# Splitting the weights of the w_a and w_b projections two output tiles at a time

## The chip, the cores and the metric

The kernel runs on one core of one Trainium2 chip. Its time is the device time of the whole program in microseconds (us), the median of several runs. A profile is one execution of the program, recorded instruction by instruction. TensorE is PE there (PEld is its weight load, which overlaps), VectorE is DVE, ScalarE is ACT, SyncE is SP; SP issues nearly all loads.

## The reference, cut to what matters

A two-layer encoder over 512 tokens of width 1024, in float32. In each layer a normed input is projected, four attention heads and four recurrent heads run on it, and their outputs, 512 wide each, are projected back to 1024, gated, added and projected once more:

```python
for layer in range(DEPTH):                       # 2
    h = rmsnorm(x, attn_norm[layer])
    proj = h @ w_in[layer]
    (a_q, a_k, a_v, b_q, b_ff, b_fb, b_i, b_g, gate_a, gate_b) = split_columns(proj)
    y_a = diff_attention(a_q, a_k, a_v, ...) @ w_a[layer]              # w_a: 512 x 1024
    y_b = hgrn2_bidirectional(b_q, b_ff, b_fb, b_i, b_g, ...) @ w_b[layer]   # w_b: 512 x 1024
    merged = jax.nn.sigmoid(gate_a) * y_a + jax.nn.sigmoid(gate_b) * y_b
    x = x + merged @ w_o[layer]                                        # w_o: 1024 x 1024
    h = rmsnorm(x, ffn_norm[layer])
    x = x + (jax.nn.silu(h @ w_gate[layer]) * (h @ w_up[layer])) @ w_down[layer]
return rmsnorm(x, final_norm)
```

## The kernel before, in words

Every large product is made of three matmuls. A float32 operand is split into hi, rounded to the type in which TensorE takes it at full rate, and lo, the rest; `mm3` (lines 207 to 210) adds hi x hi, hi x lo and lo x hi into one PSUM bank. So weights come in three steps. `wload` issues the DMA of up to 2048 columns per partition into a buffer `raw` (two of them). `wsplit` rounds a part of it with ScalarE into `hi` (line 92) and subtracts with VectorE into `lo` (line 81). Then TensorE reads both. The pool of `hi` and `lo` has three buffers each of 128 x 1024, whatever part of them a split fills; a split that needs a fourth waits until TensorE has read the oldest for the last time.

`project_fm` computes output tiles of 128 features x 512 tokens, each in one of four banks (`mbank`, in the trace `m`). With eight blocks of rows (k=8: w_in, w_o) a tile's weights are 8 x 128 = 1024 columns, one full split buffer. With four blocks of rows (k=4: w_a and w_b, whose inputs are 512 wide) they are 512 columns, half a buffer. There are eight such tiles in w_a and eight in w_b, in each of the two layers.

The order of the work is set by the framework's scheduler. It lays the program's instructions out on the engines by their data, their buffers and a priority; what stands under `urgent()` (loads, splits, evictions) goes ahead of the rest. Each engine then runs its list strictly in that order. Within a layer, while the attention runs head by head, TensorE fills in with the second half of gate_b, with w_b (input `obh`, `obl`), with gate_a (input `hh`, `hl`), and at the end with w_a.

The steps at the end of the attention, for the last head: the values' product `ao` (12 matmuls), its square `hsq` and that square's split `sqh`, `sql`, two matmuls with ones into `hss` (lines 398 and 401) that sum it, two activations on `hsq`, the scaling by VectorE (line 84), and the split of the head into `oah` and `oal`. `w_a` sums over the four heads, so each of its tiles has nine matmuls on heads 0 to 2 and three on head 3.

`merge` evicts a tile of w_a: VectorE multiplies it into `ga`, adds that to `gb`, and splits the sum into `mh` (ScalarE) and `ml` (VectorE). These are the eight blocks of rows of w_o, which starts next; its first tiles need `mh` and `ml` of tile 0, and each one all eight in the end.

Of the kernel before, what the change touches and what calls it, by code (L numbers as in the profile page):

```python
# [18 lines left out]
P = 128  # L19
# [28 lines left out]
def kernel(  # L48
# [19 lines left out]
    urgent = tc.high_priority  # L68
# [22 lines left out]
    def split_act(src, hi, lo):  # L91
        return ACT.copy(hi, src), tt(lo, src, hi.bitcast(F32), ALU.subtract)  # L92
# [14 lines left out]
    def bank(name="s"):  # L107
        return pside.tile([P, T], F32, tag="s", name=name)

    def mbank(name="m"):  # L110
        return pm.tile([P, T], F32, tag="m", name=name)
# [76 lines left out]
    def wload(src):  # L188

        _, k, c = src.shape  # L190
        raw = wp.tile([P, 2048], F32, tag="raw", name="raw")
        v = raw[:, :k * c].rearrange("p (k c) -> p k c", c=c)
        load(v, src)
        return v

    def wsplit(v):

        _, k, c = v.shape
        hi = hp.tile([P, 1024], F32R, tag="hi", name="hi")[:, :k * c].rearrange("p (k c) -> p k c", c=c)
        lo = hp.tile([P, 1024], F32R, tag="lo", name="lo")[:, :k * c].rearrange("p (k c) -> p k c", c=c)  # L200
        split_act(v, hi, lo)
        return hi, lo

    def rows(w, k0, nk, c0, n):
        return w[k0 * P:(k0 + nk) * P, c0:c0 + n].rearrange("(k p) c -> p k c", p=P)

    def mm3(ps, lh, ll, rh, rl, start, stop):
        PE.matmul(ps, lh, rh, start=start, stop=False)  # L208
        PE.matmul(ps, lh, rl, start=False, stop=False)  # L209
        PE.matmul(ps, ll, rh, start=False, stop=stop)  # L210

    def project_fm(w, cols, evac, k=DC, ah=None, al=None):

        ah = hh if ah is None else ah
        al = hl if al is None else al
        width = 2048 // k
        i = 0
        while i < len(cols):
            n = 1
            while n * P < width and i + n < len(cols) and cols[i + n] == cols[i] + n * P:  # L220
                n += 1
            with urgent():
                raw = wload(rows(w, 0, k, cols[i], n * P))
            for j in range(n):
                with urgent():
                    wh, wl = wsplit(raw[:, :, j * P:(j + 1) * P])
                ps = mbank()
                for c in range(k):
                    mm3(ps, wh[:, c, :], wl[:, c, :], ah[:, c, :], al[:, c, :], c == 0, c == k - 1)
                with urgent():  # L230
                    evac(i + j, ps)
            i += n
# [30 lines left out]
    with tc.tile_pool(name="init", bufs=1, reuse_waits="tile") as ip:  # L263
# [4 lines left out]
        with urgent():  # L268
            ACT.dma_start(vecs, small)
            for c in range(DC):  # L270
                if c % 4 == 0:
                    raw = wp.tile([P, 2048], F32, tag="raw", name="raw").rearrange("p (k d c) -> p k d c", k=4, d=2)
# [9 lines left out]
        for c in range(DC):  # L282
            with urgent():
# [3 lines left out]
                wh, wl = hi[:, c % 2], lo[:, c % 2]  # L287
# [8 lines left out]
            for i in range(4):  # L296
                cs = slice(i % 2 * P, (i % 2 + 1) * P)
# [6 lines left out]
        with tc.issue_after(norms[-1][1].ins):  # L304
# [53 lines left out]
            for dst, quarter in ((sin, 0.0), (cos, 0.25)):  # L358
                n = ip.tile([P, 32], F32, tag="n", name="n")
# [355 lines left out]
    for l in range(LAYERS):  # L715
        win = w_in[l]
        an = [vecs[:, V_FFN + 8 * l + c:V_FFN + 8 * l + c + 1] for c in range(DC)]
        with ExitStack() as mix:
# [14 lines left out]
            def gate_b(i0):  # L733
                project_fm(win, [G_B + (i0 + i) * P for i in range(4)], scaled(lambda i: gb[:, i0 + i, :]))
                for i in range(i0, i0 + 4):
                    sigmoid(gb[:, i, :])

            with tc.tile_pool(name=f"hgrn{l}", bufs=2, reuse_waits="tile") as hgp:
# [3 lines left out]
                def gates_in(h0):  # L742
                    for h in (h0, h0 + 1):
                        heads[h] = (hgp.tile([P, T], F32, tag="q", name="q"),
                                    hgp.tile([P, 2, T], F32, tag="z", name="z"),
                                    hgp.tile([P, T], F32, tag="sg", name="sg"))
                    if first:
                        with urgent():
                            for i, ps in enumerate(first):
                                scaled(lambda _: heads[i % 2][1][:, i // 2, :])(0, ps)  # L750
                        first.clear()
                    else:
                        for d, c0 in ((0, B_FF), (1, B_FB)):
                            project_fm(win, [c0 + h0 * P, c0 + (h0 + 1) * P],
                                       scaled(lambda i: heads[h0 + i][1][:, d, :]))
                    project_fm(win, [B_Q + h0 * P, B_Q + (h0 + 1) * P], scaled(lambda i: heads[h0 + i][0]))
# [21 lines left out]
            with tc.tile_pool(name=f"merge{l}", bufs=1, reuse_waits="tile") as gm, ExitStack() as late:  # L778
# [11 lines left out]
                with tc.tile_pool(name=f"attn{l}", bufs=1, reuse_waits="tile") as ap:  # L790
# [6 lines left out]
                               k=4, ah=obh, al=obl)  # L797
# [24 lines left out]
        with tc.tile_pool(name=f"ffn{l}", bufs=2, reuse_waits="tile") as fp:  # L822
            gh = fp.tile([P, FC, T], F32R, name="gh", bufs=1)
            gl = fp.tile([P, FC, T], F32R, name="gl", bufs=1)
            for f0 in range(0, FC, 2):
# [3 lines left out]
                for f in (f0, f0 + 1):  # L829
                    c0 = slice((f - f0) * P, (f - f0 + 1) * P)  # L830
                    tmp = []
                    for raw in (rg, ru):
                        with urgent():
                            wh, wl = wsplit(raw[:, :, c0])
                        ps = mbank()
# [14 lines left out]
            if l < LAYERS - 1:  # L850
                nn = [vecs[:, V_ATT + 8 * (l + 1) + c:V_ATT + 8 * (l + 1) + c + 1] for c in range(DC)]
                for c0 in range(0, DC, 2):
                    ps = [mbank(), mbank()]
                    for k0, nk in groups:
                        with urgent():
                            raw = wload(rows(w_down[l], k0, nk, c0 * P, 256))
                        for j in range(2):
                            with urgent():
                                wh, wl = wsplit(raw[:, :, j * P:(j + 1) * P])
# [10 lines left out]
            else:  # L870
# [10 lines left out]
                ps = [[mbank(), mbank()] if t < 2 else [bank(), bank()] for t in range(TC)]  # L881
# [3 lines left out]
                for k, t, half in order:  # L885
                    if k not in sp:
                        with urgent():
                            if k % 2 == 0:
                                raw = wload(rows(w_down[l], k, 2, 0, D))
                            sp[k] = wsplit(raw[:, k % 2:k % 2 + 1, :])  # L890
                    wh, wl = sp[k]
                    tok, cs = slice(t * P, (t + 1) * P), slice(half * 512, (half + 1) * 512)
# [55 lines left out]
```

## Time and profile before

| | us |
|---|---|
| median of 3 runs | 1623.28 |
| lowest and highest run | 1622.96, 1624.02 |
| the profiled execution: its time | 1623.66 |
| the profiled execution: its span, first to last instruction | 1621.9 |
| TensorE busy | 1602.1 |
| VectorE busy | 1013.1 |
| ScalarE busy | 771.6 |

The mean granted TensorE clock of the profiled execution is 0.999. A row of the timeline gives the start of an instruction from the span's start, its duration, engine, line, operation, output <- inputs by the program's names, and in brackets how long the engine had stood idle and what ended that. Matmuls overlap: one lasts 0.39 us, and the next starts before it ends. A row of the waits gives who waited for whom, the total, how many times, and the longest. A row of a window gives busy time and count of each engine in a stretch.

### The profile page before, as it was taken

Reading aid. Unit: us, or ns where it says so; the run is one execution under the profiler, and the core shown is the slowest. Engines: PE = TensorE matmul, PEld = TensorE weight load, DVE = VectorE, ACT = ScalarE, POOL = GpSimd, SP = SyncE. Lnnn points to the kernel's source line nnn. Section 1 sums busy time; section 2 is a strip of 40 time slices with the busy share of each in tenths; the row PEclk is TensorE's granted clock in tenths of the full one; section 3 lists DMA queues with packets and bytes.
Section 4 is the critical chain, followed back from the end, with each engine's and each line's share of the span. In section 5 each row is a group of like instructions: output and inputs, shape, how many; then the busy total and the mean of one; then the engine's idle time right before and its main releaser. Section 6 shows DMA issues by size and latency. Waiting matters only on the chain.

```text
span 1621.9 us, 18719 instructions
## 1 busy us (share of the span) xinstructions
PE 1602.1 (99%) x7456; PEld 1323.5 (82%) x7456; DVE 1013.1 (62%) x1636; ACT 771.6 (48%) x1186; POOL 8.1 (1%) x21
## 2 busy tenths in 40 slices
PE   8999999999999999999999999999999999999998
PEld 6888888887888888888888888888878888888886
DVE  8878977877654444433368789788875444444224
ACT  4666666676432323322355667676754323233213
POOL 2000000000000000000000000000000000000000
PEclk9999999999999999999999999999999999999999
DMA  5312212221333223323322222122123233332221
GB/s 189 105 52 79 79 61 70 78 79 52 104 104 92 90 83 99 111 89 100 103 92 83 73 78 79 54 77 79 52 79 97 84 104 104 104 103 92 104 85 72
DMA packets 117927, 142.53 MB, mean 88 GB/s; under 512 B 3152, under 2 KB 100432, under 8 KB 117840
## 3 DMA queue, kind: packets, MB, share of 16 engines
q1 hardware_dynamic: 117152, 140.78, 26.8%
q8 instruction: 58, 0.95, 0.2%
q10 hardware_dynamic: 688, 0.56, 0.1%
q14 instruction: 29, 0.24, 0.0%
HBM read 139.23 MB, written 2.10 MB: 87 GB/s over the span
## 4 chain that ended last, share of the span: by engine, by line
PE 83%; DVE 11%; ACT 4%; issue 1%; DMA 0%; ACTq 0%; DVEq 0%
PE m L210 24%; PE m L208 24%; PE m L209 24%; DVE lo L81 2%; DVE fl L81 2%; PE sc L542 2%; PE s L208 1%; PE s L209 1%; PE s L210 1%; DVE z L81 1%; PE qk L659 1%; PE wt L706 1%; PE po L593 1%; PE qk L656 1%; DVE cum L447 1%
## 5 line engine op out<-in xcount | busy, mean ns | idle before, releaser
L92 ACT CAST hi<-raw 128x1024 fp32r<-128x1024 f32 (+2 forms) x274 | 272.2, 995 | 616.4 <-PE m L209 477.2
L208 PE MATMUL m<-hh,hi 128*128 128x512 f32 x1216 | 476.5, 392 | 5.7 <-DVE hi L289 5.7
L210 PE MATMUL m<-hh,lo 128*128 128x512 f32 x1216 | 476.2, 392 | 0.0
L209 PE MATMUL m<-hl,hi 128*128 128x512 f32 x1216 | 476.1, 392 | 0.0
L81 DVE TENSOR_TENSOR lo<-raw,hi 128x1024 fp32r<-128x1024 f32 (+2 forms) x282 | 320.9, 1139 | 177.5 <-ACT hi L92 176.1
L208 PEld LDWEIGHTS m<-hh,hi 128*128 128x128 f32 x1216 | 228.9, 188 | 52.2 <-ACT sacc L78 5.7
L209 PEld LDWEIGHTS m<-hl,hi 128*128 128x128 f32 x1216 | 228.9, 188 | 47.3 <-DVE hl L84 0.4
L210 PEld LDWEIGHTS m<-hh,lo 128*128 128x128 f32 x1216 | 228.9, 188 | 47.1 <-DVE lo L81 0.3
L81 DVE TENSOR_TENSOR gu<-m,rbc 128x512 f32<-128x512 f32 x88 | 60.9, 692 | 241.2 <-PE m L210 237.2
L208 PE MATMUL m<-hi,hh 128*128 128x512 f32 x256 | 101.4, 396 | 0.0
L209 PE MATMUL m<-lo,hh 128*128 128x512 f32 x256 | 100.9, 394 | 0.0
L210 PE MATMUL m<-hi,hl 128*128 128x512 f32 x256 | 100.9, 394 | 0.0
L78 ACT ACTIVATE fl<-fl 128x1024 f32<-128x1024 f32 (+1 forms) x56 | 48.5, 872 | 43.8 <-DVE fl L81 43.8
L210 PE MATMUL m<-gh,lo 128*128 128x512 f32 x176 | 68.5, 389 | 0.0
L209 PE MATMUL m<-gl,hi 128*128 128x512 f32 x176 | 68.5, 389 | 0.0
L208 PE MATMUL m<-gh,hi 128*128 128x512 f32 x176 | 68.5, 389 | 0.0
L210 PEld LDWEIGHTS m<-hi,hl 128*128 128x128 f32 x256 | 48.2, 188 | 9.6
L542 PEld LDWEIGHTS sc<-fl 128*128 128x128 f32 x384 | 49.0, 191 | 8.5 <-DVE fl L81 4.3
L209 PEld LDWEIGHTS m<-lo,hh 128*128 128x128 f32 x256 | 48.2, 188 | 9.3
L208 PEld LDWEIGHTS m<-hi,hh 128*128 128x128 f32 x256 | 48.2, 188 | 9.3
L542 PE MATMUL sc<-fl 128*128 128x128 f32 x384 | 51.5, 277 | 2.8 <-DVE fl L81 2.6
L209 PE MATMUL m<-ml,hi 128*128 128x512 f32 x128 | 49.8, 392 | 0.0
(255 smaller groups left out, 2340.4 us busy)
## 6 DMA issues: line engine op xcount, KB each, us to landing
raw<-in_w_in_dram SPq DMA_DIRECT2D x46, 1024.0 KB, 5.0
raw<-in_w_gate_dram SPq DMA_DIRECT2D x22, 1024.0 KB, 5.1
raw<-in_w_up_dram SPq DMA_DIRECT2D x22, 1024.0 KB, 5.1
raw<-in_w_down_dram SPq DMA_DIRECT2D x19, 1024.0 KB, 4.9
raw<-in_w_o_dram SPq DMA_DIRECT2D x8, 1024.0 KB, 4.9
raw<-in_w_b_dram SPq DMA_DIRECT2D x4, 1024.0 KB, 5.0
raw<-in_w_a_dram SPq DMA_DIRECT2D x4, 1024.0 KB, 5.0
raw<-in_w_down_dram SPq DMA_DIRECT2D x4, 768.0 KB, 4.2
```

The lines of the kernel that those rows point to most:

```text
L78: return ACT.activation(o, i, func, **kw)
L81: return DVE.tensor_tensor(o, a, b, op)
L92: return ACT.copy(hi, src), tt(lo, src, hi.bitcast(F32), ALU.subtract)
L208: PE.matmul(ps, lh, rh, start=start, stop=False)
L209: PE.matmul(ps, lh, rl, start=False, stop=False)
L210: PE.matmul(ps, ll, rh, start=False, stop=stop)
L447: DVE.tensor_tensor_scan(row, seg, row, 0.0, ALU.mult, ALU.add)
L542: mm = PE.matmul(ps[:, c], K[:, c], Q[:, c], start=True, stop=True)
L593: mm = PE.matmul(po[:, tok], a, b, start=i == 0, stop=i == len(terms) - 1)
L656: mm = PE.matmul(ps[c], q2[:, c, tok], ka[:, c, :], start=True, stop=False)
L659: PE.matmul(ps[c], q2[:, c, tok], kb[:, c, :], start=False, stop=True)
L706: tr = PE.transpose(pt[:, s * P:(s + 1) * P], w[:, 0, s * P:(s + 1) * P], ident)
```

## The change

For a projection with k blocks of rows, `pair` is the number of output tiles whose weights fill a split buffer: 1 for k=8, 2 for k=4. The split is made once for `pair` tiles, and each tile's matmuls read their half of it. For k=8 nothing changes. For w_a and w_b four splits of 128 x 1024 stand in place of eight of 128 x 512.

```diff
         width = 2048 // k
+        pair = 1024 // (k * P)
         i = 0
@@
             for j in range(n):
-                with urgent():
-                    wh, wl = wsplit(raw[:, :, j * P:(j + 1) * P])
+                if j % pair == 0:
+                    with urgent():
+                        whs, wls = wsplit(raw[:, :, j * P:min(j + pair, n) * P])
+                cs = slice(j % pair * P, (j % pair + 1) * P)
                 ps = mbank()
                 for c in range(k):
-                    mm3(ps, wh[:, c, :], wl[:, c, :], ah[:, c, :], al[:, c, :], c == 0, c == k - 1)
+                    mm3(ps, whs[:, c, cs], wls[:, c, cs], ah[:, c, :], al[:, c, :], c == 0, c == k - 1)
```

The number of matmuls and loads is the same. The scheduler, however, lays out the stretch from the second attention step to the start of w_o anew, in both layers alike; the rest of the program keeps its order. Lines behind the changed ones stand three lower (398 becomes 401, 401 becomes 404). Two places follow, both of layer 0.

The first is TensorE at the end of the attention, between the last `ao` and the first matmul on head 3. Before, from the second sum (L401) on:

```order
L401 MATMUL hss<-sql,ones_r 128x512
L210 MATMUL m<-oah,lo 128x512
L208 MATMUL m<-oah,hi 128x512
L209 MATMUL m<-oal,hi 128x512
L210 MATMUL m<-oah,lo 128x512
L208 MATMUL m<-oah,hi 128x512
L209 MATMUL m<-oal,hi 128x512
L210 MATMUL m<-oah,lo 128x512
L208 MATMUL m<-oah,hi 128x512
L209 MATMUL m<-oal,hi 128x512
L210 MATMUL m<-oah,lo 128x512
L208 MATMUL m<-oah,hi 128x512 x3
```

The ten rows after L401 are w_a on heads 0 to 2; the three in the last row are the first on head 3, one for each of three tiles. Ahead of L401 stand two more of w_a, the first sum, and six of w_a behind the last `ao`. Now the whole stretch, from the last `ao` on:

```order
L210 MATMUL ao<-wh,avl 128x512
L208 MATMUL m<-oah,hi 128x512
L209 MATMUL m<-oal,hi 128x512
L210 MATMUL m<-oah,lo 128x512
L401 MATMUL hss<-sqh,ones_r 128x512
L404 MATMUL hss<-sql,ones_r 128x512
L208 MATMUL m<-oah,hi 128x512 x4
```

Three matmuls of w_a are left between the last `ao` and the first sum, none behind it, and four tiles instead of three wait for head 3. The other matmuls on heads 0 to 2 stand ahead of the last `ao` now.

The second place is the start of w_o. On VectorE, before, with `lo` of w_o's first three blocks (3567, 3600, 3637):

```order
L81 TENSOR_TENSOR lo_3567<-raw_3564,hi_3566 128x1024
L81 TENSOR_TENSOR gb_410<-gb_410,ga_3113 128x512
L81 TENSOR_TENSOR ml_3391<-gb_410,mh_3390 128x512
L81 TENSOR_TENSOR ga_3113<-ga_3113,m_3526 128x512
L81 TENSOR_TENSOR lo_3600<-raw_3564,hi_3599 128x1024
L81 TENSOR_TENSOR gb_410<-gb_410,ga_3113 128x512
L81 TENSOR_TENSOR ga_3113<-ga_3113,m_3547 128x512
L81 TENSOR_TENSOR lo_3637<-raw_3634,hi_3636 128x1024
L81 TENSOR_TENSOR gb_410<-gb_410,ga_3113 128x512
L81 TENSOR_TENSOR ml_3391<-gb_410,mh_3390 128x512 x5
```

Now, from the block before the third one (its numbers are 3568 and 3605):

```order
L81 TENSOR_TENSOR lo_3568<-raw_3532,hi_3567 128x1024
L81 TENSOR_TENSOR gb_410<-gb_410,ga_3097 128x512
L81 TENSOR_TENSOR ml_3375<-gb_410,mh_3374 128x512
L81 TENSOR_TENSOR ga_3097<-ga_3097,m_3515 128x512
L81 TENSOR_TENSOR lo_3605<-raw_3602,hi_3604 128x1024
L81 TENSOR_TENSOR gb_410<-gb_410,ga_3097 128x512
L81 TENSOR_TENSOR ml_3375<-gb_410,mh_3374 128x512 x7
```

One part of `ml` instead of three stands ahead of the third block's `lo`, and seven instead of five behind it. TensorE there, from w_a's last tile (m_3515) on; m_3538, m_3571 and m_3608 are the first three tiles of w_o:

```order
L209 MATMUL m_3515<-oal_2080,hi_3494 128x512
L210 MATMUL m_3515<-oah_2079,lo_3495 128x512
L208 MATMUL m_3538<-mh_3374,hi_3534 128x512
L208 MATMUL m_3571<-mh_3374,hi_3567 128x512
L208 MATMUL m_3608<-mh_3374,hi_3604 128x512
L209 MATMUL m_3538<-ml_3375,hi_3534 128x512
L210 MATMUL m_3538<-mh_3374,lo_3535 128x512
L208 MATMUL m_3538<-mh_3374,hi_3534 128x512
L209 MATMUL m_3571<-ml_3375,hi_3567 128x512
L210 MATMUL m_3571<-mh_3374,lo_3568 128x512
L209 MATMUL m_3538<-ml_3375,hi_3534 128x512
```

hi_3604 takes over the buffer of hi_3494, which w_a's last tile reads until the first of these rows; the last row is the first that needs the second part of `ml`. Before, TensorE took the first three blocks of rows of w_o's first tile, nine matmuls in order, ahead of any other tile, and the third tile only after the first two were done.

## The prediction

> **What bounds the kernel now.** I read the page first, then the waits of TensorE, then the windows around the places that the change touches, and last their timeline.
>
> ```profile
> PE 1602.1 (99%) x7456; PEld 1323.5 (82%) x7456; DVE 1013.1 (62%) x1636; ACT 771.6 (48%) x1186; POOL 8.1 (1%) x21
> PE 83%; DVE 11%; ACT 4%; issue 1%; DMA 0%; ACTq 0%; DVEq 0%
> ```
>
> TensorE is busy 99% of the span, and the chain that ended last runs mostly through it. A change that adds no matmul can therefore change the time only by opening or closing gaps between matmuls. What one matmul costs in a full stream I take from two rows nine matmuls into the same stretch, and the gaps that exist from TensorE's waits:
>
> ```profile
> 386.39 0.39 PE L208 MATMUL m<-oah,hi 128*128 128x512 f32 x1
> 388.20 0.39 PE L210 MATMUL m<-oah,lo 128*128 128x512 f32 x1
> PE m L208 <- DVE hi L289: 5.7, 1, 5.7
> PE sc L542 <- DVE fl L81: 2.6, 3, 1.3
> PE m L210 <- DVE lo L81: 1.8, 2, 0.9
> PE m L208 <- ACT oah L92: 1.2, 2, 0.6
> PE qk L659 <- DVE kb L81: 0.3, 2, 0.2
> ```
>
> From 386.39 to 388.20 there are eight steps: one matmul of 512 columns costs TensorE 0.227 us. Of the waits, the first two lie at the start and in the recurrence, which the change leaves alone. The third and fourth, once in each layer, lie at the w_a projection. So the most that can be won is small, and what can be lost is any stretch where TensorE has nothing independent to do. The windows show where that is already near:
>
> ```profile
> core 0: us, PE busy (x) PEld busy (x) DVE busy (x) ACT busy (x) POOL busy (x), PEclk, DMA share, GB/s
> 272.00:371.60 99.60, 99.48 (x473) 81.40 (x472) 82.67 (x147) 71.84 (x139) 0.00 (x0) 1.00 0.19 64
> 383.40:389.20 5.80, 5.19 (x22) 3.57 (x20) 1.46 (x3) 3.16 (x5) 0.00 (x0) 1.00 0.01 3
> 389.20:394.00 4.80, 3.92 (x16) 2.79 (x17) 3.97 (x7) 2.28 (x4) 0.00 (x0) 1.00 0.00 0
> 394.00:406.20 12.20, 12.20 (x54) 10.10 (x55) 11.99 (x19) 6.14 (x9) 0.00 (x0) 1.00 0.53 173
> 406.20:412.00 5.80, 5.80 (x26) 4.52 (x25) 5.72 (x9) 2.20 (x3) 0.00 (x0) 1.00 0.54 181
> ```
>
> In layer 0 the attention (272 to 371.6) is full. The gaps are in the two windows from 383.4 to 394, where the last attention head is normalised and w_a waits for it. That the waits for lo and oah count 2 each says that layer 1 repeats it.
>
> **The splits themselves.** Sixteen weight blocks are now rounded and subtracted at 1024 columns in place of 32 at 512.
>
> ```profile
> L81 DVE TENSOR_TENSOR lo<-raw,hi 128x1024 fp32r<-128x1024 f32 x234 | 286.0, 1222 | 143.8 <-ACT hi L92 142.3
> L92 ACT CAST hi<-raw 128x1024 fp32r<-128x1024 f32 x234 | 246.0, 1051 | 558.5 <-PE m L209 419.4 <-PE s L210 83.0 <-issue 31.0
> L81 DVE TENSOR_TENSOR lo<-raw,hi 128x512 fp32r<-128x512 f32 x40 | 27.3, 686 | 0.0
> L92 ACT CAST hi<-raw 128x512 fp32r<-128x512 f32 x32 | 19.5, 620 | 22.1 <-PE m L209 22.0
> ```
>
> ScalarE saves 16 x (2 x 0.620 - 1.051) = 3.0 us, VectorE 16 x (2 x 0.686 - 1.222) = 2.4 us. I cost this at nothing: the work is hidden under TensorE, which is busy 99.48 of 99.60 us where most of these blocks are made. Where that cover is thin it can turn into a loss, since one split now holds ScalarE 0.43 and VectorE 0.54 us longer in front of the attention's own steps. Inside the attention by the new order TensorE has 5 to 42 independent matmuls (1.1 to 9.5 us) in front of nearly every step that could be late, so I take 0 there, between a gain of 0.15 us per layer (the kb wait, 0.3 over both layers) and a loss of 1.5 us per layer (about three of the seven pairs exposed at 0.54).
>
> **The end of attention.** What the order moves is the filler: matmuls of w_a on heads 0 to 2, which TensorE can do while head 3 is finished. Before, three split buffers hold three output tiles, 27 matmuls of filler. Now they hold six tiles, of which the four banks let four begin, 36 matmuls. But most of them stand earlier. Between the last matmul of the values and the first one that needs head 3 there were 6, 2 and 10 (ahead of sqh's sum, between the two sums, behind them); now there are 3, 0 and 0. What they covered is this chain, in layer 0:
>
> ```profile
> 383.37 0.39 PE L210 MATMUL ao<-wh,avl 128*128 128x512 f32 x1
> 383.80 0.60 ACT L78 ACTIVATE hsq<-ao 128x512 f32<-128x512 f32 x1 [2.05 <-PE ao L210]
> 384.43 0.62 ACT L391 CAST sqh<-hsq 128x512 fp32r<-128x512 f32 x1
> 385.08 0.69 DVE L81 TENSOR_TENSOR sql<-hsq,sqh 128x512 fp32r<-128x512 f32 x1 [4.22 <-ACT sqh L391]
> 385.10 0.50 PE L398 MATMUL hss<-sqh,ones_r 128*128 128x512 f32 x1
> 385.90 0.42 PE L401 MATMUL hss<-sql,ones_r 128*128 128x512 f32 x1
> 386.36 0.69 ACT L78 ACTIVATE hsq<-hss,fixed 128x512 f32<-128x512 f32 x1 [1.32 <-PE hss L401]
> 387.08 0.63 ACT L78 ACTIVATE hsq<-hsq 128x512 f32<-128x512 f32 x1
> 387.75 0.75 DVE L84 SCALAR_TENSOR_TENSOR hsq<-ao,dgain,hsq 128x512 f32<-128x512 f32 x1 [1.98 <-ACT hsq L78]
> 388.54 0.62 ACT L92 CAST oah<-hsq 128x512 fp32r<-128x512 f32 x1 [0.82 <-DVE hsq L84]
> 389.21 0.97 PE L208 MATMUL m<-oah,hi 128*128 128x512 f32 x3 [0.62 <-ACT oah L92]
> ```
>
> Each row starts as the one before it ends; the chain can't be shortened by filler. From 383.37 it gives sqh's sum at 385.10, the second sum when sql ends (385.82), and the first matmul with head 3 another 389.21 - 385.90 = 3.31 us later, 5.76 us in all. Before, TensorE put 21 matmuls (1 + 6 + 1 + 2 + 1 + 10 = 4.77 us) into 5.84 us and lost 1.07. Now it has 6 (1.36 us) for 5.76 and loses 4.40: 0.8 ahead of the first sum, 0.5 between them, 3.1 behind.
>
> Behind head 3 something is won. Before, tile 3 of w_a could be split only after a buffer came free, and that split queued behind VectorE's evictions:
>
> ```profile
> 390.70 1.88 DVE L81 TENSOR_TENSOR ga<-ga,m 128x512 f32<-128x512 f32 x3 [0.83 <-PE m L210]
> 393.85 0.49 PE L210 MATMUL m<-oah,lo 128*128 128x512 f32 x1 [0.88 <-DVE lo L81]
> 406.24 0.39 PE L208 MATMUL m<-mh,hi 128*128 128x512 f32 x1
> ```
>
> From 389.21 to 406.24 are 17.03 us with 69 matmuls (15.66 us): 1.37 lost. Now tiles 4 and 5 are split before head 3 arrives. Their first bank is freed by the first eviction, 389.2 + 1.5 + 0.2 (one more matmul ahead) + 0.7 = 391.6, before TensorE wants it at 392.0 (four tiles x three matmuls later). The split for tiles 6 and 7 ends 7.7 us after head 3 by VectorE's queue (four evictions, three additions, one more eviction at 0.60 each, then the split) and is wanted after 8.7. So nothing is lost there but 0.1 us for the first matmul behind a wait. Sum: 4.40 + 0.10 against 1.07 + 1.37, a loss of 2.1 us per layer.
>
> **The start of w_o.** The late buffer now lands on w_o. Its third block's hi has to wait until w_a's last pair is read, and TensorE's third matmul of w_o uses that block. Of ml, seven of eight parts now stand behind that block's lo on VectorE. The rows of before show the steps:
>
> ```profile
> 405.78 0.39 PE L209 MATMUL m<-oal,hi 128*128 128x512 f32 x1
> 406.25 1.05 ACT L92 CAST hi<-raw 128x1024 fp32r<-128x1024 f32 x1 [1.14 <-PE m L209]
> 407.34 1.23 DVE L81 TENSOR_TENSOR lo<-raw,hi 128x1024 fp32r<-128x1024 f32 x1
> 408.48 0.69 DVE L81 TENSOR_TENSOR gb<-gb,ga 128x512 f32<-128x512 f32 x1
> 409.08 3.09 DVE L81 TENSOR_TENSOR ml<-gb,mh 128x512 fp32r<-128x512 f32 x5
> ```
>
> Let B be the issue of w_a's last matmul that reads hi (405.78 there). The cast starts at B + 0.47 and ends at B + 1.52; TensorE wants the block at B + 0.91. lo starts at about B + 1.7 (VectorE's queue by the same count of rows), the addition 1.14 later, ml's second part 0.60 after that, ending at B + 4.1. TensorE wants it as its eleventh matmul, at B + 2.3, and gets it at B + 4.2; later parts come every 0.60 us, faster than the 0.68 us of three matmuls. Lost: 1.9 plus 0.1, against 0.1 before (the window from 406.2 shows no idle time). That is 1.9 us per layer; its ends are 0, if ml comes in time after all, and 2.5, if ScalarE's mh casts (0.62 each) hold the hi.
>
> **The sum.** (2.1 + 1.9) x 2 layers = 8.0 us on the profiled execution of 1623.66, 1631.7. That execution stands 0.38 above the median of the runs, 1623.28, so I forecast 1631.3 us, 0.5% slower. 0.2% (3.2 us) is about what a measurement of this kernel tells from no change.
>
> **The rivals.** *TensorE slows down after the gap.* The first matmuls of the program start further apart than 0.227 us:
>
> ```profile
> 5.73 0.77 PE L208 MATMUL m<-hh,hi 128*128 128x512 f32 x1 [5.73 <-DVE hi L289]
> 9.57 0.40 PE L210 MATMUL m<-hh,lo 128*128 128x512 f32 x1
> ```
>
> There are nine matmuls from the one to the other, eight steps in 3.84 us, which is 2.0 us more than at full speed. If a gap of 3.1 us brings that state back, once per layer, the time is 1631.3 + 4.0 = 1635.3. For it: the new gap is more than twice the longest wait in mid-run, 1.3 us (before sc, above). Against it: behind that wait the chip shows no such phase, and the gap is interrupted by the two sums. [...] Chance 0.12.
>
> *Faster.* The wait for lo at 393.85 goes and nothing takes its place, because TensorE still has filler behind the sums. It takes at least 3.31 / 0.227, 15 matmuls there; then all 2.4 us per layer go, 1623.28 - 4.9 = 1618.4. For it: nine matmuls of filler were added and the row of the wait is real. Against it: the order has none of them there, and TensorE issues in order. Chance 0.04.
>
> *No change.* w_o starts as before, because its third block or ml is in time, and the end of attention loses half of the 2.1: 1623.28 + 2.1 = 1625.4. For it: both terms are differences between short stretches laid end to end. Against it: the chain's rows leave no slack. Chance 0.09, 0.08 of it within 0.2%.
>
> *More is lost.* The wider splits delay the attention as well, 1.5 us per layer: 1634.3. TensorE's order leaves as few as five matmuls ahead of some steps. Chance 0.08.
>
> **How the numbers follow.** The forecast keeps 0.67. Its own range is 1627.5 (w_o loses nothing: 2.1 x 2) to 1632.5 (w_o at 2.5). Adding the slower cases with their sum, I give 1626.5 to 1637.0. Faster 0.04; within 0.2% 0.08; slower 0.88.
>
> **What would show it.** In the waits of the new profile: TensorE waiting for oah about 3 us once per layer (0.6 now), for sqh and sql 0.5 to 0.8, for hi of w_o about 0.6 and for ml about 1.2; none for lo of w_a. TensorE's busy time unchanged, the splits' groups at 250 of 1024 and none of 512 on ScalarE. The prediction is wrong if the oah wait stays under 1 us, or if w_a's first matmuls on heads 0 to 2 open gaps ahead of the values. Matmuls 0.4 to 0.5 us apart behind the oah wait would decide for the first rival.

## The result and the profile after

The changed kernel takes 1646.44 us, the median of 4 runs from 1645.96 to 1647.09. The kernel before, run beside it, takes 1623.55. The ratio is 1.0141, with a 95% interval from 1.0129 to 1.0153: 22.9 us slower. The forecast was 1631.3 us (1626.5 to 1637.0), so the sign was right, and the size was wrong by 15.1 us, nearly three times the 8.0 us foreseen.

The page of the profile after, busy time and the chain that ended last:

```profile
PE 1612.8 (98%) x7456; PEld 1330.8 (81%) x7456; DVE 1013.0 (62%) x1620; ACT 767.4 (47%) x1170; POOL 8.0 (0%) x21
PE 82%; DVE 11%; ACT 5%; issue 1%; DMA 0%; ACTq 0%; DVEq 0%
```

TensorE still runs 7456 matmuls, but it is busy 10.7 us longer than before. So about half of the loss doesn't show as idle time: matmuls themselves have become longer. The other half is in TensorE's waits (who waited for whom, total, times, longest; the rows of the start and of the recurrence are left out):

```profile
PE m L209 <- DVE ml L81: 6.6, 2, 3.3
PE m L208 <- ACT oah L92: 5.8, 2, 2.9
PE hss L401 <- ACT sqh L394: 1.3, 2, 0.7
PE qk L662 <- DVE kb L81: 1.3, 6, 0.3
PE m L208 <- ACT hi L92: 1.0, 2, 0.5
PE hss L404 <- DVE sql L81: 0.5, 2, 0.2
```

The waits for oah, sqh, sql and hi are those that the prediction named, and the wait for lo of w_a is gone. The wait for ml is 3.3 us each time, where about 1.2 was foreseen. The end of the attention in layer 0, TensorE's timeline:

```profile
390.67 0.49 PE L401 MATMUL hss<-sqh,ones_r 128*128 128x512 f32 x1 [0.66 <-ACT sqh L394]
391.39 0.50 PE L404 MATMUL hss<-sql,ones_r 128*128 128x512 f32 x1 [0.23 <-DVE sql L81]
394.77 2.08 PE L208 MATMUL m<-oah,hi 128*128 128x512 f32 x4 [2.88 <-ACT oah L92]
396.64 0.63 PE L209 MATMUL m<-oal,hi 128*128 128x512 f32 x1
397.07 0.63 PE L210 MATMUL m<-oah,lo 128*128 128x512 f32 x1
...
399.20 0.63 PE L209 MATMUL m<-oal,hi 128*128 128x512 f32 x1
399.63 0.63 PE L210 MATMUL m<-oah,lo 128*128 128x512 f32 x1
```

Behind the wait for oah the rows start 0.43 us apart and last 0.63, against 0.227 and 0.39 in a full stream. That is no wait: no bracket stands behind these rows. The windows of the same place give the reason in the column PEclk, the granted clock:

```profile
core 0: us, PE busy (x) PEld busy (x) DVE busy (x) ACT busy (x) POOL busy (x), PEclk, DMA share, GB/s
388.90:394.80 5.90, 2.13 (x8) 0.97 (x7) 1.49 (x3) 3.15 (x5) 0.00 (x0) 0.88 0.00 0
394.80:400.00 5.20, 5.20 (x12) 4.11 (x13) 2.58 (x4) 1.18 (x2) 0.00 (x0) 0.50 0.00 0
```

From 394.8 to 400 TensorE is busy without a break, and does 12 matmuls where 23 would fit, at half the clock. Then the start of w_o, TensorE's rows and below them VectorE's:

```profile
411.07 0.61 PE L208 MATMUL m<-mh,hi 128*128 128x512 f32 x2
412.19 0.51 PE L208 MATMUL m<-mh,hi 128*128 128x512 f32 x1 [0.50 <-ACT hi L92]
416.00 0.79 PE L209 MATMUL m<-ml,hi 128*128 128x512 f32 x1 [3.30 <-DVE ml L81]
416.59 0.63 PE L210 MATMUL m<-mh,lo 128*128 128x512 f32 x1
...
420.27 0.60 PE L210 MATMUL m<-mh,lo 128*128 128x512 f32 x1
420.70 0.41 PE L208 MATMUL m<-mh,hi 128*128 128x512 f32 x1
420.94 0.39 PE L209 MATMUL m<-ml,hi 128*128 128x512 f32 x1
```

```profile
411.12 0.68 DVE L81 TENSOR_TENSOR ml<-gb,mh 128x512 fp32r<-128x512 f32 x1
...
414.05 4.29 DVE L81 TENSOR_TENSOR ml<-gb,mh 128x512 fp32r<-128x512 f32 x7
```

One part of ml is ready at 411.80, before TensorE asks at 412.4, and yet TensorE waits until 416.00. The seven parts behind it start 0.60 apart, so the third of them ends at 414.05 + 2 x 0.60 + 0.69 = 415.94. That one, not the part made at 411.12, is what TensorE's first matmul with ml needs. And a second stretch of slow rows follows, to 420.7.

To add up, I count as lost what TensorE took beyond 0.2272 us per matmul (the 0.227 from above with one more digit): at the end of the attention from the start of the last ao to the first matmul of w_o, and at the start of w_o over its first 110 matmuls. Layer 0 and layer 1:

| kernel | end of attention, us | start of w_o, us |
|---|---|---|
| before | 2.42, 2.42 | 0.15, 0.15 |
| after | 7.14, 7.11 | 6.68, 6.66 |
| e1 (ml in order of blocks) | 6.84, 6.20 | 1.07, 1.07 |
| e2 (six matmuls held back) | 3.89, 4.06 | 8.17, 6.97 |
| e3 (w_a alone) | 0.54, 0.54 | 2.18, 2.18 |
| e4 (w_a alone, ml in order) | 0.54, 0.49 | -0.01, -0.01 |
| e5 (e1 and 12 spare matmuls, counted as lost) | 4.57, 4.57 | 1.10, 1.10 |
| e6 (e1 and 5 spare matmuls, counted as lost) | 4.61, 4.60 | 1.10, 1.06 |
| e7 (w_b alone) | 8.03, 7.78 | 0.11, 0.11 |

From before to after that is 9.41 us more at the end of the attention and 13.04 at w_o. Ahead of the last ao another 0.25 per layer are lost (the waits for kb are 1.3 in six in place of 0.3 in two). Together that is 22.9, the difference of the spans, 1644.8 - 1621.9 = 22.9.

### The profile page after: what moved, and what is told of

Its sections match the earlier page's. It is cut to its first block, busy times and chain, and to the rows that moved or that the text cites. A ratio compares the mean times of both kernels' runs of the same rounds, so it can differ in the third digit from the quotient of the medians.

```text
span 1644.8 us, 18677 instructions
## 1 busy us (share of the span) xinstructions
PE 1612.8 (98%) x7456; PEld 1330.8 (81%) x7456; DVE 1013.0 (62%) x1620; ACT 767.4 (47%) x1170; POOL 8.0 (0%) x21
## 4 chain that ended last, share of the span: by engine, by line
PE 82%; DVE 11%; ACT 5%; issue 1%; DMA 0%; ACTq 0%; DVEq 0%
PE m L209 24%; PE m L210 24%; PE m L208 24%; DVE lo L81 2%; DVE fl L81 2%; PE sc L545 2%; PE s L210 1%; PE s L208 1%; PE s L209 1%; ACT hi L92 1%; DVE z L81 1%; PE qk L662 1%; PE po L596 1%; PE wt L709 1%; PE qk L659 1%
## 5 line engine op out<-in xcount | busy, mean ns | idle before, releaser
L92 ACT CAST hi<-raw 128x1024 fp32r<-128x1024 f32 (+1 forms) x258 | 269.5, 1045 | 620.6 <-PE m L209 483.8
L664 DVE TENSOR_REDUCE nm<-qk 128x1 f32<-128x512 f32 x64 | 41.7, 685 | 19.8 <-PE qk L662 19.6
```

Source lines behind the costliest of these rows:

```text
L664: DVE.tensor_reduce(nm[:, c:c + 1], ps[c], AX.X, ALU.max, negate=True)
```

## The experiments

Two things had to be told apart: how much of the loss is the order of ml, and whether the slow rows come from the gap before them. e1 to e4 ran beside the kernel before at 1623.63 us, e5 to e7 beside it at 1623.28.

**e1: the parts of ml in the order of their blocks.** The order constraint ties each part to the one before it. ScalarE's list stays as it was, and on VectorE, apart from the blocks of ml, two neighbouring rows per layer change places. But the scheduler also lays out TensorE's list at the start of w_o anew: 33 rows per layer differ.

```diff
+                lows = []
...
-                    split_act(gb[:, i, :], mh[:, i, :], ml[:, i, :])
+                    parts = split_act(gb[:, i, :], mh[:, i, :], ml[:, i, :])
+                    if i:
+                        behind(parts[1], lows[-1])
+                    lows.append(parts[1])
```

> The changed kernel with one addition: VectorE makes the eight parts of ml in the order of their blocks (in the changed kernel the fourth, sixth and seventh came first). The end of attention stays as it is. Theory G (gaps plus a slow phase of TensorE behind each long gap): TensorE's wait for ml at the start of w_o falls from 3.3 us to under 1.5, no matmuls 0.43 us apart follow it, w_o's start loses about 1.1 us per layer instead of 6.7, so 1646.4 - 2 x 5.6 = 1635. Rival I (idle time alone counts, the slow rows come from something else in the program): only the gap shrinks, 2 x 3.2 us, so 1640. Rival W (the wider splits themselves slow the kernel): 1646, no change.

Measured: 1634.77 us (1633.77 to 1635.38), ratio 1.0070 [1.0056, 1.0084]. TensorE's waits for ml:

```profile
PE m L209 <- DVE ml L81: 1.1, 4, 0.4
```

TensorE at the start of w_o, down to the first matmul with ml's second part:

```profile
410.68 0.61 PE L208 MATMUL m<-mh,hi 128*128 128x512 f32 x2
411.46 0.50 PE L209 MATMUL m<-ml,hi 128*128 128x512 f32 x1 [0.17 <-DVE ml L81]
...
414.40 0.50 PE L209 MATMUL m<-ml,hi 128*128 128x512 f32 x1 [0.36 <-DVE ml L81]
```

Of 6.6 us in two waits 1.1 in four are left, and no slow rows follow at w_o. Between the medians 11.7 us are won, between the profiles 12.5: 11.2 at w_o, and 1.2 at the end of the attention, where TensorE's list is the same and the half clock held fewer matmuls (in layer 1 it lasted 3.41 us in place of 6.83). Not all of the 5.6 us per layer at w_o are the order of ml itself: TensorE's third matmul there is now one with ml, and the one that waited 0.66 us for hi comes later. The rest is the wait for the part of ml that TensorE needed, and the clock that fell in it.

**e2: a smaller gap for oah.** In w_a's tile 3 the six matmuls on its second and third block are held behind the second sum. They cover part of the 3.1 us, and leave the gap ahead of the first sum wider (the lines that hand out the matmuls are left out):

```diff
-                    mm3(ps, whs[:, c, cs], ..., c == 0, c == k - 1)
+                    first_mm = mm3(ps, whs[:, c, cs], ..., c == 0, c == k - 1)
+                    if held and (i + j, c) in held:
+                        behind(first_mm, held[i + j, c])
...
-                project_fm(w_a[l], ..., merge, k=4, ah=oah, al=oal)
+                project_fm(w_a[l], ..., merge, k=4, ah=oah, al=oal, held={(3, 1): sums["h2"]})
```

> The changed kernel with six of the matmuls that w_a makes on heads 0 to 2 (its fourth tile, blocks 1 and 2) held back on TensorE until behind the second of the two sums. The same matmuls in the same total idle time, but the gap of 3.15 us behind the sums becomes about 1.8 us, and the one ahead of the sums grows from 0.8 to 1.5. Theory G, where TensorE slows down only behind an uninterrupted gap of about 3 us: the 11 matmuls 0.43 us apart behind that gap are gone, the idle time stays: 2 x 2.6 us won, 1641.2. Rival U (TensorE's speed follows its mean busy share over some us): the mean share is unchanged, the slow rows stay, 1646. Rival W: 1646.

Measured: 1642.56 us, ratio 1.0118 [1.0104, 1.0131]; the runs fall into two pairs, 1644.4 and 1640.2 to 1640.7, so the median says little. The two layers of the one profile show why. Windows at the end of the attention, layer 0 first:

```profile
391.40:393.50 2.10, 1.81 (x7) 1.27 (x8) 0.69 (x1) 0.75 (x3) 0.00 (x0) 1.00 0.00 0
393.50:395.50 2.00, 0.58 (x3) 0.16 (x1) 0.75 (x1) 1.18 (x2) 0.00 (x0) 1.00 0.00 0
395.50:399.00 3.50, 3.42 (x15) 2.85 (x16) 2.42 (x4) 1.53 (x3) 0.00 (x0) 1.00 0.00 0
...
1202.70:1205.00 2.30, 1.95 (x5) 1.34 (x6) 0.69 (x1) 0.86 (x3) 0.00 (x0) 0.74 0.00 0
1205.00:1207.00 2.00, 1.70 (x4) 0.79 (x3) 0.75 (x2) 1.15 (x2) 0.00 (x0) 0.50 0.00 0
```

The same instructions in the same order: in layer 0 the clock stays at 1.00, in layer 1 it falls. There no gap was longer than 1.50 us (1.50 ahead of the first sum, 0.50 ahead of the second). So a fall doesn't need 3 us without work, and it isn't settled by the order alone. At w_o, where every list is that of the changed kernel, 8.17 and 6.97 us are lost in place of 6.68 and 6.66; there, too, the clock fell at another point (the last 3.41 us ahead of the fall were busy to 0.29 and 0.19, in after to 0.38). The experiment therefore gave no price of the gap, and it led to e5 and e6. The two pairs of runs differ in the clock: the mean granted clock is 0.994 in both runs at 1644.4 and 0.997 in both of the others.

**e3: only w_a is paired.** `project_fm` takes `pair` as an argument, 1 unless given:

```diff
-                project_fm(w_a[l], [i * P for i in range(DC)], merge, k=4, ah=oah, al=oal)
+                project_fm(w_a[l], [i * P for i in range(DC)], merge, k=4, ah=oah, al=oal, pair=2)
```

> The change in w_a alone; w_b is split tile by tile as before. The order then leaves 6, 2 and 13 matmuls of filler at the end of attention (6, 2 and 10 before, 3, 0 and 0 with both changed). Theory G: the end of attention loses about 0.5 us per layer instead of 2.4 before and 7.1 with both; the start of w_o loses about 2.2 (ml's parts come 4, 0, 5, 6, 1), without a slow phase; 2.7 per layer against 2.6 before: 1623.5, between 1621 and 1626. Rival W (the wider splits cost by themselves, half of them are left): 1623.5 + 11 = 1635.

Measured: 1623.68 us (11 runs), ratio 1.0002 [0.9993, 1.0011]. Between the last ao and head 3 stand 21 matmuls of filler (6, 2 and 13; before, 18), the wait for lo is gone, and what is won there is paid back for ml, which is made in another wrong order:

```profile
PE m L209 <- DVE ml L81: 3.2, 2, 1.6
```

**e4: only w_a is paired, and ml is in order.** The edits of e1 and e3 together. Against e3, TensorE's list at w_o changes here, too (47 rows per layer); those of ScalarE and VectorE differ only in ml's blocks.

> The change in w_a alone, and ml's parts in the order of their blocks. Theory G: the end of attention loses 0.5 us per layer, the start of w_o 0.2, against 2.6 before: 1623.4 - 2 x 1.9 = 1619.6, faster than before by 0.2%. Rival W: 1635. If the start of w_o has another wait (third block's hi or lo), up to 1622.

Measured: 1619.23 us (1618.99 to 1619.75, 9 runs), ratio 0.9975 [0.9965, 0.9985]. This version is faster than both kernels. TensorE's five longest waits; none lies at w_a or w_o:

```profile
PE m L208 <- DVE hi L291: 6.4, 1, 6.4
PE sc L544 <- DVE fl L81: 1.9, 3, 1.1
PE nr L583 <- DVE kl L81: 0.3, 1, 0.3
PE qk L661 <- DVE kb L81: 0.3, 2, 0.2
PE kt L490 <- ACT fs L78: 0.2, 1, 0.2
```

By the table 1.9 us per layer are won at the end of the attention and 0.16 at w_o, 4.1 in all of the 4.4 measured.

**e5 and e6: the gap filled with work that nobody reads.** The kernel of e1, with 12 (e5) or 5 (e6) matmuls into a spare bank directly behind the second sum of the last head. The results of the kernel don't use them, and `sums["h2"]` is that second sum. Apart from them every engine's list is that of e1:

```diff
+                spare = bank("spare")
+                for n in range(12):
+                    with urgent():
+                        behind(PE.matmul(spare, ones_r, oah[:, 0, :], start=n == 0, stop=n == 11), sums["h2"])
                 project_fm(w_a[l], ...)
```

> The kernel of e1 (the change, with the parts of ml made in the order of their blocks), and 12 matmuls that nobody reads (ones by oah, 512 columns, into a spare bank) directly behind the second sum of the last head. They fill 12 x 0.227 = 2.7 us of the 3.1 us in which TensorE waits for oah; nothing else moves in any engine's order. Theory C (TensorE's clock falls because the window was nearly empty, and that is a loss of its own on top of the waits): the waits still last as long, but no row behind them is 0.43 us apart. e1 lost 6.84 and 6.20 us in this stretch, of which its three waits are 4.47: 2.37 + 1.73 = 4.1 us go, 1634.8 - 4.1 = 1630.7 us, and the wait for oah shrinks to 0.4. Theory N (the rows 0.43 us apart have another cause, such as banks, evictions or w_a's late weights, and would be there without the gap): 1634.8, the slow rows stay. A rival in which filler by itself delays the chain on ScalarE and VectorE gives more than 1634.8.

> As e5 with 5 matmuls that nobody reads in place of 12: 1.1 us of the 3.1 us are filled, and 2.0 us stay empty. Nothing useful is done by them, so without any fall of the clock the time is the same as with 12. If the clock needs an uninterrupted gap of about 3 us to fall, there is no fall: 1630.7. If it goes by the share of a window of 3.4 us in which TensorE is busy (falls were seen at 0.12 to 0.37, none at 0.40 and above), the emptiest window that can be laid here has 1.36 of 3.41 us busy, 0.40: no fall or a seldom one, 1630.7 to 1632.7. If it goes by the sum of the idle time around the sums (0.8 + 0.5 + 2.0 us), the slow rows stay: 1634 to 1635.

Measured: e5 1630.78 us (1630.17 to 1631.49), ratio 1.0046 [1.0031, 1.0061]; e6 1630.59 us (1630.20 to 1631.04), ratio 1.0045 [1.0030, 1.0060]. Against the kernel before in their own runs e1 lost 11.1 us and e5 7.5: work that is thrown away makes the program 3.6 us faster than e1. The window behind the gap in e1, e5 and e6, one row each in this order:

```profile
394.70:399.00 4.30, 4.30 (x10) 3.43 (x11) 1.84 (x3) 0.93 (x1) 0.00 (x0) 0.50 0.00 0
```

```profile
395.80:400.00 4.20, 4.14 (x18) 3.44 (x19) 3.14 (x6) 2.01 (x3) 0.00 (x0) 1.00 0.00 0
```

```profile
394.70:399.00 4.30, 4.29 (x19) 3.52 (x20) 3.26 (x6) 2.00 (x2) 0.00 (x0) 1.00 0.00 0
```

The clock is 0.50 behind the gap without them and 1.00 with either number of spare matmuls; 10 matmuls become 18 or 19. In e6 TensorE still waits for oah:

```profile
391.67 1.33 PE L826 MATMUL spare<-oah,ones_r 128*128 128x512 f32 x5
394.71 1.21 PE L208 MATMUL m<-oah,hi 128*128 128x512 f32 x4 [1.71 <-ACT oah L92]
```

So the slow rows aren't a matter of w_a's banks, evictions or late weights, which are the same in the three kernels, and they don't follow from the wait. They follow from a stretch in which TensorE did too little: from 388.80 to 394.70 it ran 8 matmuls in e1 and 13 in e6. The expectation that slow rows go by the sum of idle time (1634 to 1635 for e6) falls.

**e7: only w_b is paired.** As e3, with `pair=2` on the call for w_b instead.

> The change for w_b alone; w_a is split one tile at a time as before. The order then leaves no matmul of w_a between the last matmul of the values and the first on head 3, and only three tiles wait for head 3. Theory (what costs is the missing filler at the end of the attention, and the clock that falls in it): waits of 1.5 (sqh), 0.5 (sql) and 3.1 us (oah), 1.1 for lo of w_a as before, 2.6 for the clock, and 0.1 at the start of w_o, where ml's parts stand in the old order: 8.9 + 0.1 against 2.57 before, 6.4 x 2 = 13 us, 1636.5 us. Without a fall of the clock 1631.3. Rival (all of the loss comes from pairing w_a; w_b's splits only move hidden work): 1623.6.

Measured: 1637.55 us (1637.45 to 1637.76), ratio 1.0088 [1.0071, 1.0105]. TensorE's waits at the end of the attention, and those of the attention itself:

```profile
PE m L208 <- ACT oah L92: 5.7, 2, 2.9
PE hss L400 <- ACT sqh L393: 2.7, 2, 1.3
PE qk L662 <- DVE kb L81: 1.3, 6, 0.3
PE m L210 <- DVE lo L81: 0.7, 1, 0.7
PE ao L209 <- DVE wl L81: 0.5, 2, 0.2
```

Pairing w_b alone takes the filler away, and costs 14.3 us; pairing w_a alone costs nothing. The total of 1636.5 was nearly met, but by luck: its terms were off and offset each other. Ahead of the last ao 1.4 us per layer are lost, where the expectation names nothing; the waits for kb and for the split of the attention's weights (wl) are part of that. In turn the wait for lo, expected in both layers, came in one. In layer 0 12 rows ran slowly, in layer 1 only 6; that the slow matmuls of layer 0 gave VectorE the time to make lo is argued, not shown.

## Why the prediction was right in sign and wrong in size

*The splits cost nothing:* right. The forecast group stands in the profile after, and on ScalarE no weight block of 512 columns is left:

```profile
L92 ACT CAST hi<-raw 128x1024 fp32r<-128x1024 f32 x250 | 262.8, 1051 | 585.1 <-PE m L209 448.3 <-PE s L210 83.0 <-PE m L210 29.1
```

The change for w_a alone, half of the splits, leaves the time at 1.0002. What the attention lost ahead of the last ao, 0.25 us per layer, is inside the bounds set for it. In the order of e7 it is 1.4, close to the upper bound of 1.5.

*The end of the attention:* right for the waits. The chain gave 0.82, 0.50 and 3.15 us, 4.47 in sum, where 4.40 was forecast, and the wait for lo went. The matmuls of filler were moved and not lost: from the same qk of layer 0 to the last ao TensorE runs 587 in place of 563, and from there to w_o 66 in place of 90. The last ao starts 5.57 us later, at 388.94, of which 24 matmuls take 5.45. That stretch was full already, so they covered nothing there.

*The start of w_o:* hi was right, 0.66 us, and so were the times of VectorE's rows: the second part of ml that it makes ends at 414.05 + 0.69 = 414.74, and w_a's last matmul that reads hi, the B of the prediction, is issued at 410.62, so that is B + 4.1, as forecast. The failed step is the sentence "Lost: 1.9 plus 0.1", and in it the claim that TensorE first waits for ml at its eleventh matmul from B, for the second part that VectorE makes. The prediction took the first row of ml in VectorE's order for block 0 and the next for block 1. The rows name the tile but not the block. In the program as built the parts are made in the order of blocks 3, 5, 6, 0, 4, 7, 2, 1, so block 0 is the third of the last seven, and block 1 the very last. TensorE therefore waited at its first matmul with ml, the fourth of w_o: 3.58 us, until 416.00, or B + 5.4. The first matmul with block 1, at 418.40, starts just after the last part is made, at 414.05 + 4.29 = 418.34. In all the start of w_o lost 6.5 us per layer more than before, where 1.9 was forecast. With ml in order (e1) it is 0.9, but there TensorE's list is another as well, and asks for block 1 at its thirteenth matmul of w_o and not at its ninth. No run has ml in order with the list that the prediction priced.

*The clock:* the rival "TensorE slows down after the gap" was real. It was priced well, 4.0 us, against 3.6 measured between e1 and e5 and 3.9 between their profiles. The second failed step is that the forecast put this term at nothing: it held that without more matmuls the time can change "only by opening or closing gaps between matmuls", while TensorE was busy 10.7 us longer with the same matmuls. Two arguments stood against the rival. That no phase follows the wait of 1.3 us before sc was true, but says nothing on 3 us. That the two sums interrupt the gap is refuted: in after the clock fell with them in between, in both layers. And the same mechanism was not asked about at w_o, where behind the wait of 3.58 us the slow rows brought another 2.1 us per layer.

*The sum:* with the clock kept up and ml in order, the kernels of e5 and e6 come to 1630.8 and 1630.6 us, against the 1631.3 forecast without either. That the totals are so close is in part luck: w_o costs 0.9 us per layer more than before there and not 1.9, the end of the attention 2.2 where 2.1 was forecast, and about 1 us of the 7.5 and 7.3 lies in places that the forecast put at nothing. The same luck brings the rival's sum, 1635.3, near the time of e1, 1634.77. Both errors lay on the same side. The top of the range, 1637.0, lies below the forecast with both slower rivals added, 1631.3 + 4.0 + 3.0 = 1638.3, and neither of them held the order of ml.

## What to carry to other kernels

A strict order of instructions that names only buffers doesn't say which part of a tile a row makes; before a wait is priced from it, each row has to be followed to its address. When an edit frees work to run earlier, ask which stall that work was covering: here 24 matmuls that moved into a full stretch gained nothing (they took 5.45 of the 5.57 us by which the last ao starts later), and the stall that they left cost its length, 2.88 us per layer for oah, and then the clock, 6.83 us at 0.50. Where filler runs out around such a stall, even throwaway matmuls can pay (e5, 3.6 us faster than e1), but keeping real ones for it (w_a alone, ml in order, 1619.23 us) was better.

## What the runs showed of the hardware

In the trace of after, the granted clock is 1.00 or 0.50, and it changes on a grid: behind its first fall the stretches of half and full clock last 6.83, 13.65, 6.83 and 785.07 us, 2, 4, 2 and 230 times 3.413. What went ahead of a fall can be read in the 3.413 us that end at it. Counting 0.227 us for each matmul of 512 columns, TensorE was busy in this stretch, for the falls in the middle of the program, to 0.13 and 0.38 (after, at the two places), 0.26 and 0.11 (e1), 0.29, 0.40 and 0.19 (e2), 0.13 and 0.07 (e7). Of the stretches of the grid at full clock with such matmuls alone, the emptiest without a fall were at 0.41 (e6) and 0.43 (e2). So in these runs a stretch that was filled to 0.40 or less was enough, with single gaps of 1.5 and 0.5 us in it (e2). Where the grid lies against the gap differs between the layers of e2: the last ao of layer 1 starts 1201.10 - 389.74 = 811.36 us behind that of layer 0, 237.7 times 3.413. That this makes its runs fall into two pairs fits the granted clocks, 0.994 and 0.997, but only one of the four was profiled. The limit itself rests on few stretches, with e2's fall at 0.40 beside e6's 0.41 without one, and the traces can't say what the chip counts as busy.

The type of hi and lo is the faster one in these traces. In the trace of before, a matmul of 512 columns in it takes 0.227 us of a full stream, 0.44 ns per column. The eight float32 matmuls `sc` (L542) that begin at 130.16 last 1.06 us together and 0.28 each, so they follow one another by (1.06 - 0.28) / 7 = 0.11 us for 128 columns, 0.87 ns per column.
